# Adding the two directions' decay matrices on VectorE before the output matmuls of a state-space scan

## Chip, core and metric

One NeuronCore of one Trainium2 chip runs the whole kernel. The metric is the device time of one execution in microseconds (us); lower is better.

## What is computed

The kernel is one layer of a hybrid mixer on 1024 latent tokens with 256 context tokens as a prefix: one input projection, an HGRN2 branch (A), a Mamba-2 SSD branch (B), gates, an output projection and a layer norm. The change lies in branch B, where the sequence runs in both directions over chunks of 128 tokens. For each direction the reference computes, cut to what matters:

```python
cum = jnp.cumsum((dt * a_neg)...)
y_inter = jnp.einsum('bktgn,bktgr,bkgrnp->bktgrp', cc, jnp.exp(cum), s_prev)
cb = jnp.einsum('bktgn,bksgn->bktsg', cc, bc)
lmat = masked_exp(cum[:, :, :, None] - cum[:, :, None, :], causal)
y_intra = jnp.einsum('bktsg,bktsgr,bksgrp->bktgrp', cb, lmat, x_dt)
y = y_inter + y_intra          # per direction
...
y = y_f + y_b + d_skip * xh    # both directions
```

There are 16 heads of width 64 in 4 groups, and a state of 128. In `y_intra` both directions multiply the same tokens of x, each by its own matrix of 128 by 128.

## The kernel before

Projections are split-precision products: each weight tile of 128 columns is split into a high and a low part, and `mm3` (L178 to L180) issues three matmuls of 128x512 per 128 rows of contraction. These projections are also the fill work: `Fill.window` walks through the yields of a scan and after each one draws fill pieces until `due`, the yield's weight times the rate of the window, is used up. A piece counts its columns over 512, and one whole unit is 24 matmuls. The rates of the four group windows are `FILL_B`; the yield of a scan position counts `W_SCAN`, and that of a y step `W_Y`.

`b_scan` (from L793) handles one of the four groups. After the transposes and the masked product CB of B and C (L815), it makes nine positions of the state scan (xw L889 on GpSimd, bu L892 on TensorE, St L900 and L902 on VectorE), and then runs 16 y steps, two head pairs `j` times eight chunks `t`. A y step goes through four stages, at lags of 0, 2, 3 and 4 yields:

- `loads`: GpSimd issues a DMA (L837) that broadcasts the rows of cum of two heads and two directions into a tile L of 128x512.
- `exponents`: ScalarE makes e = exp(L) (L847); VectorE takes the minimum of L with CU (L848); ScalarE makes four exponentials of 128x128 in place (L851).
- `products`: GpSimd multiplies e by C (L856), VectorE multiplies L by CB (L857).
- `y_matmuls` (L859 to L875): eight matmuls into one PSUM tile yi, for k in 0..3 and the two heads h. k = 0, 1 multiply x by L of the two directions, k = 2, 3 multiply the states St by e. Heads h = 0 and 1 write different halves of 64 partitions. After four chunks VectorE adds d times x (L875).

L and e tiles share one pool of 12 buffers with other tiles, so a load waits until the matmuls of an earlier step have let a buffer go. The exact order on each engine is set by a list scheduler over this code, which takes program order, waits and priorities (`ahead`) into account. Beside the y steps the same engines serve the fill: ScalarE and VectorE split weights (L162, L163), run the convolution (L743, L746) and evacuate gates (L611, L925), and `b_out` and `b_scale` (L946 to L963) normalize the group before. ScalarE loads a function table (ACT_TABLE_LOAD) whenever the next function is not in the one it holds.

Of the kernel before, what the change touches and what calls it, by code (L numbers as in the profile page):

```python
# [14 lines left out]
NT = L // P  # L15
# [15 lines left out]
GRAIN = 512  # L31
FILL_T, FILL_A = 0.8, 0.8
GA = (2, 0, 0, 6)
FILL_B = (0.88, 0.97, 0.97, 1.05)
OUT1, OUT2 = 16, 3
GATES = (2, 1, 1, 4)
W_0, W_PRE, W_SCAN, W_Y = 1.0, 0.7, 0.35, 0.5
LAGS = (0, 2, 3, 4)
EARLY = (5, 7)
REP = 8  # L40
# [8 lines left out]
ALU = mybir.AluOpType  # L49
# [55 lines left out]
def hybrid(tc, x, c, ctx, c_ctx, w_mod, b_mod, w_in, lb_logits, a_norm_w, conv_w, conv_b, dt_bias,  # L105
# [4 lines left out]
    V, S, T, G = nc.vector, nc.scalar, nc.tensor, nc.gpsimd  # L110
# [8 lines left out]
    with root:  # L119
# [9 lines left out]
        def sc(name):  # L129
            return ps.tile([P, 512], F32, tag="sc", bufs=5, name=name)  # L130
# [602 lines left out]
        def bt_(tag, bufs, shape, name):  # L733
            return bp.tile([P] + list(shape), F32, tag=tag, bufs=bufs, name=name)
# [58 lines left out]
        def b_scan(g, u):  # L793
# [14 lines left out]
            for b in range(2):  # L808
                cb = sc(f"cb{g}_{b}")
                for i in range(4):  # L810
                    t = (b * 4 + i) * P
# [6 lines left out]
            xt = bt_("xt", 1, [NT, 2 * P], f"xt{g}")  # L818
# [34 lines left out]
            def products(j, t):  # L853
# [2 lines left out]
                G.tensor_tensor(C4, C4, Cc[:, ts].unsqueeze(1).broadcast_to([P, 4, P]), ALU.mult)  # L856
                V.tensor_tensor(Lm, Lm, CB[:, :, ts].unsqueeze(1).broadcast_to([P, 2, 2, P]), ALU.mult)  # L857

            def y_matmuls(j, t):  # L859
                Lm, Ce = Ls.pop((j, t)), Cs.pop((j, t))  # L860
                if t % 4 == 0:
                    yis[j] = sc(f"yi{g}_{j}_{t // 4}")
                yi = yis[j]
                o = slice((t % 4) * P, (t % 4 + 1) * P)
                for k in range(4):
                    for h in range(2):
                        hs = slice((2 * j + h) * 64, (2 * j + h + 1) * 64)
                        if k < 2:
                            a, r = xt[:, t, hs], Lm[:, h, k, :]
                        else:  # L870
                            a, r = St[:, t if k == 2 else NT - 1 - t, k - 2, hs], Ce[:, h, k - 2, :]
                        T.matmul(yi[h * 64:(h + 1) * 64, o], a, r, start=(k == 0), stop=(k == 3))  # L872
                if t % 4 == 3:
                    bs = slice((t - 3) * P, (t + 1) * P)
                    V.scalar_tensor_tensor(y[:, j, bs], xc[:, j, bs], bd_col(2 * g + j), yi, ALU.mult, ALU.add)  # L875


            St = bt_("St", 1, [NT, 2, 256], f"St{g}")
# [28 lines left out]
            for k in range(len(EARLY), len(steps) + LAGS[-1]):  # L907
                for lag, stage in zip(LAGS, (loads, exponents, products, y_matmuls)):
                    if 0 <= k - lag < len(steps):
                        stage(*steps[k - lag])  # L910
                yield W_Y
# [4 lines left out]
        def z_proj(g, u):  # L916
            for j in range(2):
                blk = 2 * g + j
                for t0, n, acc in (proj_k if blk == 2 * BG - 1 else proj)(O_Z + blk * P, parts_l, f"z{blk}"):
                    if acc is None:  # L920
                        yield n / GRAIN / 4
                        continue
                    with ahead():
                        zs = bt_("gb", 4, [512], f"z{blk}_{t0}")
                        S.activation(zs, acc, AF.Silu)  # L925
                    if g + 1 < BG:
                        z_mul(u, j, t0, zs)
                    else:
                        z_last.append((u, j, t0, zs))
                    yield n / GRAIN / 4  # L930
# [39 lines left out]
        def b_window(g):  # L970
            scan = b_scan(g, ub_[g])
            if g:
                yield from islice(scan, OUT1)
                yield from b_out(g - 1, ub_[g - 1])
                yield from islice(scan, OUT2)
                b_scale(g - 1, ub_[g - 1])
            yield from scan
# [11 lines left out]
        for g in range(BG):  # L989
# [9 lines left out]
            else:  # L999
                fill.add(z_proj(g, ub_[g]), f"z{g}")  # L1000
            fill.window(b_window(g), FILL_B[g])
            fill.until(f"b{g + 1}")
# [33 lines left out]
        with ExitStack() as st:  # L1036
# [40 lines left out]
            for nh in range(2):  # L1077
# [9 lines left out]
                for t in range(NT):  # L1087
# [8 lines left out]
                    r, bs = rr[t], st_[t]  # L1096
# [36 lines left out]
```

## Time and profile before

| what | us |
|---|---|
| median of the three runs | 1261.88 |
| the runs | 1260.83, 1261.88, 1946.27 |
| the profiled execution | 1258.42 |
| its span in the trace | 1256.6 |

The median is what a later time is compared with. The trace belongs to the profiled execution, which is 3.46 us under that median, and 1.8 us of it lie outside the span of the trace.

### The profile page before, as it was taken

The numbers are of one execution on the slowest core, as the hardware profiler recorded it, in microseconds if no ns is written. First come the engines' busy times: TensorE is split into PE (matmuls) and PEld (weight loads), VectorE is DVE, ScalarE is ACT, GpSimd is POOL, SyncE is SP. The second block draws the span as 40 slices with busy tenths as digits, with TensorE's granted clock in tenths as the row PEclk, the third lists the DMA queues.
The fourth block names the chain that finished last, engine by engine and source line by source line (L and its number), as shares of the span: only waits on it lengthen the run. The fifth ranks groups of instructions, "written<-read, shape, count | busy, mean of one in ns | idle before, by whom it ended". The sixth has DMA issues, their size and how long they took to land.

```text
span 1256.6 us, 18683 instructions
## 1 busy us (share of the span) xinstructions
PE 1225.9 (98%) x7624; PEld 994.4 (79%) x7624; DVE 775.4 (62%) x988; ACT 580.2 (46%) x926; POOL 197.1 (16%) x200
## 2 busy tenths in 40 slices
PE   5999999999999999999999999999999999999997
PEld 2778888788888888888788878877887778888885
DVE  2437744934644742569687677758765755575468
ACT  2436244434324323346954586467858862222010
POOL 1130000000000000005414261425053410000000
PEclk8999999999999999999999999999999999999999
DMA  9611212102112223113402241224233316654312
GB/s 317 201 42 49 53 35 94 44 18 69 35 34 70 60 68 111 51 34 93 135 26 59 68 151 33 69 71 140 82 104 110 126 51 234 241 211 141 119 42 101
DMA packets 115444, 119.14 MB, mean 95 GB/s; under 512 B 10320, under 2 KB 94992, under 8 KB 115360
## 3 DMA queue, kind: packets, MB, share of 16 engines
q1 hardware_dynamic: 105568, 101.04, 25.2%
q0 software_dynamic: 9440, 16.87, 4.7%
q8 instruction: 60, 0.98, 0.3%
q14 instruction: 24, 0.20, 0.1%
q10 hardware_dynamic: 352, 0.05, 0.0%
HBM read 98.77 MB, written 19.14 MB: 94 GB/s over the span
## 4 chain that ended last, share of the span: by engine, by line
PE 86%; ACT 5%; DVE 4%; issue 2%; DMA 1%; POOL 1%; SPq 0%; DVEq 0%; ACTq 0%; POOLq 0%
PE x L178 6%; PE x L179 5%; PE x L180 5%; PE yi L872 4%; PE f L180 3%; PE f L178 3%; PE f L179 3%; PE bu L892 2%; PE ga L178 2%; PE pl L520 2%; PE fo L180 2%; PE fo L179 2%; PE fo L178 2%; PE ga L180 2%; PE ga L179 2%; PE pb L179 2%
## 5 line engine op out<-in xcount | busy, mean ns | idle before, releaser
L856 POOL TENSOR_TENSOR e<-e,C 128x512 f32<-128x512 f32 x64 | 91.0, 1429 | 103.4 <-ACT e L847 103.0
L889 POOL TENSOR_TENSOR xw<-xtc,WU 128x512 f32<-128x512 f32 x8 | 8.7, 1112 | 584.3 <-ACT xtc L826 584.3
L851 ACT ACTIVATE L<-L,BIA 128x128 f32<-128x128 f32 x256 | 80.8, 390 | 36.8 <-DVE L L848 36.4
L848 DVE TENSOR_TENSOR L<-L,CU 128x512 f32<-128x512 f32 x64 | 77.3, 1231 | 9.6 <-ACT e L847 9.5
L857 DVE TENSOR_TENSOR L<-L,CB 128x512 f32<-128x512 f32 x64 | 55.5, 871 | 19.9 <-ACT L L851 19.6
L746 DVE SCALAR_TENSOR_TENSOR xc<-x,par,xc 128x496 f32<-128x496 f32 (+1 forms) x64 | 47.1, 735 | 21.4 <-ACT xc L743 20.3
L512 ACT COPY KX<-K 128x1024 f32<-128x1024 f32 x28 | 32.0, 1141 | 50.3 <-DVE K L531 45.2
L562 DVE SCALAR_TENSOR_TENSOR S<-S,T,ub 128x128 f32<-128x128 f32 x64 | 22.2, 347 | 51.4 <-ACT S L558 27.7
L178 PE MATMUL fo<-wo,mh 128*128 128x512 f32 x128 | 50.2, 392 | 0.0
L180 PE MATMUL fo<-wo,mh 128*128 128x512 f32 x128 | 49.8, 389 | 0.0
L179 PE MATMUL fo<-wo,ml 128*128 128x512 f32 x128 | 49.8, 389 | 0.0
L531 DVE TENSOR_TENSOR K<-K,T 128x1280 f32<-128x1280 f32 x28 | 46.4, 1658 | 3.4 <-ACT KX L512 1.6
L872 PEld LDWEIGHTS yi<-L,xt 128*64 128x64 f32 x512 | 26.7, 136 | 26.5 <-issue 18.9
L872 PE MATMUL yi<-L,xt 128*64 128x128 f32 x512 | 42.1, 285 | 3.5 <-issue 1.8
L837 POOL DMA_DIRECT2D L<-cum_d x64 | 39.7, 621 | 25.5 <-PE yi L872 10.8
L847 ACT ACTIVATE e<-L 128x512 f32<-128x512 f32 x64 | 37.4, 620 | 8.4 <-PE bu L892 3.9
L746 DVE SCALAR_TENSOR_TENSOR B<-x,par,B 128x496 f32<-128x496 f32 (+1 forms) x32 | 23.6, 736 | 28.5 <-ACT B L743 24.4
L533 DVE TENSOR_TENSOR Q<-Q,T 128x1024 f32<-128x1024 f32 x28 | 37.6, 1344 | 2.9 <-PE pl L520 2.9
L872 PE MATMUL yi<-e,St 128*64 128x128 f32 x512 | 38.9, 273 | 0.0
L520 PEld LDWEIGHTS pl<-Q,KX 128*64 128x64 f32 x896 | 30.1, 138 | 9.5 <-issue 8.7
L523 DVE COPY_PREDICATED PD<-mk,pl 128x512 f32<-128x512 uint8 x24 | 17.7, 739 | 27.9 <-PE pl L520 27.8
L520 PE MATMUL pl<-Q,KX 128*64 128x64 f32 x896 | 34.1, 230 | 0.7 <-DVE Q L533 0.7
(995 smaller groups left out, 3742.7 us busy)
## 6 DMA issues: line engine op xcount, KB each, us to landing
L<-cum_d POOLq DMA_DIRECT2D x64, 256.0 KB, 4.1
wm<-in_w_mod_dram SPq DMA_DIRECT2D x16, 512.0 KB, 8.2
xt<-in_x_dram SPq DMA_DIRECT2D x8, 512.0 KB, 8.2
ga_d<-ga SPq DMA_DIRECT2D x16, 256.0 KB, 2.0
gb_d<-gb SPq DMA_DIRECT2D x16, 256.0 KB, 3.9
m<-ga_d SPq DMA_DIRECT2D x8, 512.0 KB, 4.9
gbt<-gb_d SPq DMA_DIRECT2D x8, 512.0 KB, 6.7
wg<-in_w_mod_dram SPq DMA_DIRECT2D x8, 512.0 KB, 5.0
```

Source lines behind the costliest of these rows:

```text
L178: T.matmul(dst, ah, bh, start=(first and i == 0), stop=False)
L179: T.matmul(dst, al, bh, start=False, stop=False)
L180: T.matmul(dst, ah, bl, start=False, stop=(last and i == n - 1))
L520: T.matmul(pl[rows_, t * HP:(t + 1) * HP], KX[:, o:o + HP], qx, start=True, stop=True)
L531: V.tensor_tensor(kv, kv, sub(Ta, lv, [[w, NA // w], [NA - lv, 2], [0, lv]]), ALU.mult)
L746: V.scalar_tensor_tensor(d3[:, :, a:z], r3[:, :, a + o:z + o], cw_col(t, blk), d3[:, :, a:z], ALU.mult, ALU.add)
L837: G.dma_start(t_[:].rearrange("p a b c -> p (a b c)"), bass.AP(src.tensor, src.offset, [[NQT * BH * 2 * QT, REP], [0, P // REP], [1, 4 * Q ...
L848: V.tensor_tensor(Lm, Lm, sub(CU[:], t * BH + h0, [[1, 2], [NT * BH, 2], [0, P]]), ALU.min)
L851: S.activation(Lm[:, h, d, :], Lm[:, h, d, :], AF.Exp, bias=BIA[:, d, t, h0 + h:h0 + h + 1])
L856: G.tensor_tensor(C4, C4, Cc[:, ts].unsqueeze(1).broadcast_to([P, 4, P]), ALU.mult)
L857: V.tensor_tensor(Lm, Lm, CB[:, :, ts].unsqueeze(1).broadcast_to([P, 2, 2, P]), ALU.mult)
L872: T.matmul(yi[h * 64:(h + 1) * 64, o], a, r, start=(k == 0), stop=(k == 3))
```

## The change

The product L times CB is followed by one more VectorE instruction, which adds the two directions' halves of L (128x2x128 elements) in place. `y_matmuls` now runs k in 0..2: first the two products of St and e, then one product of x with the sum. Each y step thus has 6 matmuls where it had 8 (in the trace each of them stands as two instructions, so 12 for 16). The product of C with exp(cum) stays on GpSimd. The weight of a y step and the fill rates are changed as well.

```diff
-FILL_B = (0.88, 0.97, 0.97, 1.05)
+FILL_B = (0.85, 0.94, 0.94, 1.02)
-W_0, W_PRE, W_SCAN, W_Y = 1.0, 0.7, 0.35, 0.5
+W_0, W_PRE, W_SCAN, W_Y = 1.0, 0.7, 0.35, 0.54
...
                 V.tensor_tensor(Lm, Lm, CB[:, :, ts].unsqueeze(1).broadcast_to([P, 2, 2, P]), ALU.mult)
+                V.tensor_tensor(Lm[:, :, 0, :], Lm[:, :, 0, :], Lm[:, :, 1, :], ALU.add)
...
-                for k in range(4):
+                for k in range(3):
                     for h in range(2):
                         hs = slice((2 * j + h) * 64, (2 * j + h + 1) * 64)
                         if k < 2:
-                            a, r = xt[:, t, hs], Lm[:, h, k, :]
+                            a, r = St[:, NT - 1 - t if k else t, k, hs], Ce[:, h, k, :]
                         else:
-                            a, r = St[:, t if k == 2 else NT - 1 - t, k - 2, hs], Ce[:, h, k - 2, :]
-                        T.matmul(yi[h * 64:(h + 1) * 64, o], a, r, start=(k == 0), stop=(k == 3))
+                            a, r = xt[:, t, hs], Lm[:, h, 0, :]
+                        T.matmul(yi[h * 64:(h + 1) * 64, o], a, r, start=(k == 0), stop=(k == 2))
```

In the changed file the lines after the added one stand two lower (L872 is L874, L953 is L955), and the added instruction is L859.

TensorE, group 1, the step of j = 0 and t = 5. L and e are the step's tiles, xt the tokens of x, St the states, and gb and x are fill. Before:

```order
L180 MATMUL gb_512_5917<-hl_95,gb2h 128x512
L872 MATMUL yi_0_1_5941<-L_0_5_5764,xt_5432 64x128 x4
L872 MATMUL yi_0_1_5941<-e_0_5_5899,St_5494 64x128 x4
L178 MATMUL x_0_5996<-hh_80,x4h 128x512
L179 MATMUL x_0_5996<-hh_80,x4l 128x512
```

Now:

```order
L180 MATMUL x_0_5951<-hl_89,x4h 128x512
L874 MATMUL yi_0_1_5929<-e_0_5_5888,St_5478 64x128 x4
L874 MATMUL yi_0_1_5929<-L_0_5_5742,xt_5416 64x128 x2
L178 MATMUL x_0_5951<-hh_82,x4h 128x512
L179 MATMUL x_0_5951<-hh_82,x4l 128x512
```

The L matmuls moved behind the four of e, and two of them are gone. Over the whole program TensorE has 6093 matmuls where it had 6221; the 64 steps stood in 64 unbroken runs and stand in 72, since fill now comes between the e and the L matmuls of some steps.

VectorE, the same place. Before:

```order
L857 TENSOR_TENSOR L_0_4_5725<-L_0_4_5725,CB_5398 128x512
L848 TENSOR_TENSOR L_0_5_5764<-L_0_5_5764,CU 128x512
L848 TENSOR_TENSOR L_0_6_5863<-L_0_6_5863,CU 128x512
L875 SCALAR_TENSOR_TENSOR xc_5042<-xc_5042,par,yi_0_0_5736 128x512
L963 SCALAR_TENSOR_TENSOR xc_4242<-xc_4242,par,sq_1_1_5855 128x512
L857 TENSOR_TENSOR L_0_5_5764<-L_0_5_5764,CB_5398 128x512
L857 TENSOR_TENSOR L_0_6_5863<-L_0_6_5863,CB_5398 128x512
```

Now:

```order
L857 TENSOR_TENSOR L_0_4_5701<-L_0_4_5701,CB_5382 128x512
L965 SCALAR_TENSOR_TENSOR xc_4242<-xc_4242,par,sq_1_1_5838 128x512
L848 TENSOR_TENSOR L_0_5_5742<-L_0_5_5742,CU 128x512
L859 TENSOR_TENSOR L_0_4_5701<-L_0_4_5701 128x2x128
L848 TENSOR_TENSOR L_0_6_5852<-L_0_6_5852,CU 128x512
L965 SCALAR_TENSOR_TENSOR xc_4242<-xc_4242,par,sq_1_1_5838 128x512
L877 SCALAR_TENSOR_TENSOR xc_5035<-xc_5035,par,yi_0_0_5713 128x512
L857 TENSOR_TENSOR L_0_5_5742<-L_0_5_5742,CB_5382 128x512
L859 TENSOR_TENSOR L_0_5_5742<-L_0_5_5742 128x2x128
L857 TENSOR_TENSOR L_0_6_5852<-L_0_6_5852,CB_5382 128x512
```

The add L859 follows its product L857 directly, or with one instruction between.

ScalarE, group 1, where `b_out` of group 0 (sq and bss) meets the step of t = 4. Before:

```order
L847 ACTIVATE e_0_4_5865<-L_0_4_5725 128x512
L953 ACT_TABLE_LOAD
L953 ACTIVATE sq_0_1_5840<-bss_0_5850,epsr 128x512
L953 ACTIVATE sq_1_1_5855<-bss_1_5859,epsr 128x512
L954 ACT_TABLE_LOAD
L954 ACTIVATE sq_0_1_5840<-sq_0_1_5840 128x512
L954 ACTIVATE sq_1_1_5855<-sq_1_1_5855 128x512
L851 ACTIVATE L_0_4_5725<-L_0_4_5725,BIA 128x128 x4
L847 ACTIVATE e_0_5_5899<-L_0_5_5764 128x512
```

Now:

```order
L847 ACTIVATE e_0_4_5854<-L_0_4_5701 128x512
L955 ACT_TABLE_LOAD
L955 ACTIVATE sq_0_1_5823<-bss_0_5833,epsr 128x512
L956 ACT_TABLE_LOAD
L956 ACTIVATE sq_0_1_5823<-sq_0_1_5823 128x512
L851 ACTIVATE L_0_4_5701<-L_0_4_5701,BIA 128x128 x3
L955 ACT_TABLE_LOAD
L955 ACTIVATE sq_1_1_5838<-bss_1_5848,epsr 128x512
L851 ACT_TABLE_LOAD
L851 ACTIVATE L_0_4_5701<-L_0_4_5701,BIA 128x128
L956 ACTIVATE sq_1_1_5838<-sq_1_1_5838 128x512
L847 ACTIVATE e_0_5_5888<-L_0_5_5742 128x512
```

The two halves' logarithm and exponential no longer go together, which makes four table loads of two; group 2 shows the same. Over the whole program ScalarE has 109 table loads where it had 97, the added ones 4, 4, 2 and 2 in the windows of groups 0 to 3.

## Rows read from the trace of the kernel before

**Rows 1.** Page, span, and busy time, share and instructions of each engine

```profile
span 1256.6 us, 18683 instructions
PE 1225.9 (98%) x7624; PEld 994.4 (79%) x7624; DVE 775.4 (62%) x988; ACT 580.2 (46%) x926; POOL 197.1 (16%) x200
```

**Rows 2.** Busy time by stretch, the y steps of the four groups

```profile
core 0: us, PE busy (x) PEld busy (x) DVE busy (x) ACT busy (x) POOL busy (x), PEclk, DMA share, GB/s
597.00:655.00 58.00, 58.00 (x437) 44.62 (x436) 42.82 (x48) 42.29 (x85) 20.30 (x20) 1.00 0.29 87
724.00:778.00 54.00, 52.81 (x393) 40.92 (x394) 43.15 (x53) 44.25 (x85) 22.89 (x22) 1.00 0.34 103
846.00:901.00 55.00, 52.47 (x394) 40.68 (x393) 44.22 (x53) 44.47 (x85) 22.07 (x21) 1.00 0.36 110
965.00:1020.00 55.00, 54.76 (x384) 41.36 (x384) 40.65 (x38) 47.59 (x87) 20.10 (x19) 1.00 0.40 125
sum 222.00, PE 218.04 PEld 167.58 DVE 170.85 ACT 178.60 POOL 85.36; mean PE 54.51 PEld 41.89 DVE 42.71 ACT 44.65 POOL 21.34
```

**Rows 3.** Waits for line L872: TensorE idle until VectorE's product, us and times

```profile
  DVE L L857: 5.5, 8
```

**Rows 4.** Timeline of TensorE, one y step of group 0: start, us, what, count

```profile
621.98 0.39 PE L180 MATMUL x<-hl,x2h 128*128 128x512 f32 x1
622.30 0.66 PE L872 MATMUL yi<-L,xt 128*64 128x128 f32 x8
622.79 0.61 PE L872 MATMUL yi<-e,St 128*64 128x128 f32 x8
623.33 0.50 PE L178 MATMUL x<-hh,x2h 128*128 128x512 f32 x1
623.66 0.40 PE L179 MATMUL x<-hh,x2l 128*128 128x512 f32 x1
```

**Rows 5.** Chain that ended last, in time: a fill matmul, then 20 transposes

```profile
562.20 0.23 PE x L180
562.43 2.18 PE bx L825 x20
```

**Rows 6.** Page, groups of the y step's instructions: busy, mean ns, idle before

```profile
L856 POOL TENSOR_TENSOR e<-e,C 128x512 f32<-128x512 f32 x64 | 91.0, 1429 | 103.4 <-ACT e L847 103.0
L848 DVE TENSOR_TENSOR L<-L,CU 128x512 f32<-128x512 f32 x64 | 77.3, 1231 | 9.6 <-ACT e L847 9.5
L857 DVE TENSOR_TENSOR L<-L,CB 128x512 f32<-128x512 f32 x64 | 55.5, 871 | 19.9 <-ACT L L851 19.6
```

**Rows 7.** Line L848: ns min, median and max of its 64 instructions

```profile
L848 DVE TENSOR_TENSOR L<-L,CU x64: 673/692/3994, 576.9 to 1007.2; 128x512 f32<-128x512 f32 x64
```

**Rows 8.** Groups by shape on VectorE: the same operation at 512 and 1024 elements

```profile
L338 DVE TENSOR_TENSOR hl<-hm,hh 128x512 fp32r<-128x512 f32 x8 | 5.5, 690 | 0.2
L163 DVE TENSOR_TENSOR ml<-m,mh 128x1024 fp32r<-128x1024 f32 x8 | 9.8, 1226 | 0.3 <-ACT mh L162 0.3
```

**Rows 9.** Groups in 560:1060: one of ScalarE's groups of table loads

```profile
L851 ACT ACT_TABLE_LOAD x21 | 26.9, 1283 | 0.3
```

**Rows 10.** Timeline of ScalarE in group 1, from the logarithm of group 0

```profile
723.92 0.63 ACT L847 ACTIVATE e<-L 128x512 f32<-128x512 f32 x1
724.57 1.28 ACT L953 ACT_TABLE_LOAD   x1
725.87 1.26 ACT L953 ACTIVATE sq<-bss,epsr 128x512 f32<-128x512 f32 x2
...
739.38 0.63 ACT L847 ACTIVATE e<-L 128x512 f32<-128x512 f32 x1 [0.86 <-POOL e L856]
...
750.95 1.28 ACT L851 ACTIVATE L<-L,BIA 128x128 f32<-128x128 f32 x4 [0.92 <-DVE L L848]
...
755.94 1.28 ACT L851 ACTIVATE L<-L,BIA 128x128 f32<-128x128 f32 x4 [3.19 <-DVE L L848]
```

**Rows 11.** Timeline of VectorE in group 1: the product of t = 5

```profile
736.34 0.69 DVE L857 TENSOR_TENSOR L<-L,CB 128x512 f32<-128x512 f32 x1 [1.66 <-ACT L L851]
```

**Rows 12.** Timeline of TensorE in group 1: the matmuls of t = 5

```profile
737.47 0.66 PE L872 MATMUL yi<-L,xt 128*64 128x128 f32 x8
```

## Prediction

> **What bounds the kernel now.** I began with the page's busy shares. TensorE is busy 1225.9 of 1256.6 us, VectorE 62% and ScalarE 46% [rows 1]. The end of the program is therefore set by TensorE's stream, and an instruction taken from it is worth its own slot as long as nothing makes TensorE wait. The second view, busy time by stretch, tells whether that holds where the change lies. In the four stretches of y steps, 222.0 us together, TensorE is busy 218.04 us at the full granted clock (1.00, the 2.4 GHz level), but the helpers are far busier than over the whole program: ScalarE 178.6 us (80%), VectorE 170.85 us (77%) [rows 2]. The third view, the waits of the y matmuls, shows the coupling: TensorE sits idle until VectorE's product L857 only 8 times in 64 steps, 5.5 us in all [rows 3]. So TensorE bounds, and VectorE and ScalarE stand close behind it in these stretches.
>
> **TensorE: what is removed.** The trace shows each y matmul as two instructions. A step starts its L part at 622.30, its e part at 622.79 and the next fill matmul at 623.33 [rows 4]: eight L instructions take 0.49 us, 61 ns each. Half of them go, 4 x 61 = 0.245 us a step, and 64 steps give 15.7 us. A slot, not the duration of 0.66 us that the row prints, is the price, since the instructions overlap. It cannot be read from matmuls that use all output columns: the 20 transposes of 128 columns take 2.18 us, 109 ns each [rows 5]. The y matmuls of the two heads write different halves and run nearly side by side; since a whole pair is removed and pairs remain, 61 ns is the price of one. What bounds it from both sides are these two rows: 61 ns (15.7 us) and 109 ns (27.9 us). I take the first, which is the row of the very instructions.
>
> **TensorE: what is added.** The program's order has 72 runs of y matmuls where it had 64. Entering a run costs 622.30 - 621.98 = 0.32 us where a fill matmul follows its neighbour by 0.23 [rows 4, 5], and leaving it 623.66 - 623.33 = 0.33, again 0.10 more. A further run thus costs 0.19 us, and 8 of them 1.6 us. TensorE's stream becomes 15.7 - 1.6 = 14.1 us shorter.
>
> **The fill rates** add or remove no work, they move it. A unit of fill is 24 matmuls of 0.23 us, 5.5 us. Per y step the due work goes from 0.88 x 0.5 = 0.44 units to 0.85 x 0.54 = 0.459 in group 0, from 0.485 to 0.508 in groups 1 and 2, from 0.525 to 0.551 in group 3: 0.10, 0.12, 0.12 and 0.14 us a step. Over 16 steps in each group 8.0 us of fill go from the scan positions to the y steps. The y stretches become 222.0 - 15.7 + 1.6 + 8.0 = 215.9 us long. Should the fill run out before the last step, steps would stand back to back. In group 3 the window's yields weigh 15.67 (5.55 up to the scan's end, 18 y yields of 0.54, 0.4 of `b_out`), times 1.02 is 15.98 units of 16 at hand, where it was 15.70; it just suffices, so I cost it at nothing.
>
> **VectorE: the add.** No row shows a TENSOR_TENSOR of 256 elements. 512 elements take 690 ns and 1024 take 1226 [rows 8], 1.05 ns an element, so 256 take about 0.42 us when nothing disturbs. Disturbed it is longer: L848 has a median of 692 ns and a mean of 1231, with one of 3994, and its neighbour L857, of the same shape, a mean of 871 [rows 6, 7]. So a y step's VectorE instruction loses 0.18 us (L857) to 0.54 us (L848) on average; the add costs 0.42 at least, 0.60 like its neighbour, 0.96 like L848. A bound below nothing is excluded, since it replaces no other VectorE instruction. I take 0.60, since L859 stands directly behind L857 in the order. 64 adds are then 38.4 us (27 to 61). VectorE's load in the y stretches becomes 170.85 + 38.4 = 209.3 of 215.9 us: it fits, with hardly anything to spare. In the order the added instruction delays what is queued behind it, the next L848 and L857, and by them ScalarE's L851.
>
> The cover of the add is the new order of the matmuls. L is now needed after the e part, 0.49 us later than before. Where TensorE waited for the product already, 8 steps, an add of 0.60 shows by 0.60 - 0.49 = 0.11 us, 0.9 us in all. The step at 737.47 has 0.44 us to spare after its product, which ends at 736.34 + 0.69 [rows 11, 12], and becomes one of that kind; GpSimd's e products, which now come first, I cost at nothing: GpSimd is busy 85 of the 222 us [rows 2], and no wait for it is among those of the y matmuls.
>
> What disturbs L848 is told by the trace only as durations. The Trainium skill, SBUF — State Buffer, section "Who interferes with whom", states that a VectorE instruction with two SBUF inputs contends with a GpSimd one that reads SBUF, and that the loser waits for the whole instruction. The long L848 agree. By that rule the add, with both inputs in SBUF, can wait for a whole L856; the rule speaks against the change, and the last rival below is its result.
>
> **ScalarE: the table loads.** The order holds 12 further table loads, at 1.283 us each [rows 9]. A load at 724.57 follows the instruction that started at 723.92 and lasted 0.63, and the next starts at 725.87 [rows 10]: a switch costs 1.30 us and nothing more. Whether it shows depends on ScalarE's gaps. From 723.92 to 750.0 in group 1 it has one gap of 0.86 us, then 0.92 and 3.19 [rows 10]; the two loads added there, between logarithm and exponential, are 2.6 us ahead of the step at 737.47 with its 0.44 us. I let them show in full, and likewise in group 2, where the order is the same: 2 x 2.6 = 5.1 us. The other eight lie in group 0, where no TensorE time is lost now [rows 2], or at the windows' ends, and I cost them at nothing; uncovered they are 10.3 us.
>
> The Trainium skill, ScalarE: Activation LUTs, section "What ACT_TABLE_LOAD costs", gives 2.66 us for a switch, with a drain behind the load. The trace does not agree here: 1.30 us from load to next start. By the page these four loads would be 10.6 us in place of 5.1, and I go by the row.
>
> **The sum.** -15.7 + 1.6 + 5.1 + 0.9 = -8.1 us. The profiled execution took 1258.42 us, so 1250.3; its median of runs lies 3.46 higher, and so do I: 1253.8 us.
>
> **Rivals.**
> *All covered.* Of the 222 us, 51 us of VectorE's and 43 us of ScalarE's time are idle [rows 2]. If neither term shows, the gain is TensorE's 14.1 us: 1247.8 us. Against it stand ScalarE's unbroken stretch and the small slack in rows 11 and 12.
> *ScalarE paces the steps.* All 12 loads show, 15.4 us against 14.1: 1263.2 us, no change. For it speaks ScalarE's 80%; against it that groups 0 and 3 lose 0.24 us of TensorE time together now [rows 2].
> *VectorE becomes the bound.* If each add costs what L848 loses, 0.96 us, VectorE needs 170.85 + 61.4 = 232.3 us in stretches that could be 215.9, and TensorE waits for the 16.4 us: 1261.88 - 14.1 + 16.4 = 1264.2 us, slower than before. It decides from (215.9 + 14.1 - 170.85) / 64 = 0.92 us an add. For it: L848's mean. Against it: L857, two places nearer, loses a third of that, and waiting for GpSimd can't grow beyond GpSimd's own 85 us.
> *The removed matmuls are worth a full slot.* At 109 ns the gain is 27.9 - 1.6 = 26.3 us, 1235.6 us. Rows 4 speak against it. That the change does not do what it says is excluded by the order: 128 matmuls fewer.
>
> **How the numbers follow.** Forecast 0.48; all covered 0.25; ScalarE 0.13; VectorE 0.12; full slot 0.02. The predicted time is the forecast's, 1253.8 us. The range runs from 1245 (all covered, with the adds' and loads' bounds at nothing and 3 us of TensorE's present waits gone) to 1266 (past both slower cases), and leaves out the full slot and a pileup of both slower cases. About 2% is what a measurement of this kernel can tell from no change, 25 us: faster by that is only the full slot, 0.02; slower would need VectorE's case at twice its price, 0.03; within it 0.95.
>
> **What would show it.** In the changed profile L874 should have 512 e and 256 L instructions with slots of 61 ns; L859 a mean of 0.4 to 1.0 us; TensorE's idle time in the y stretches 4 us before and about 10 after, most of it in groups 1 and 2 and released by L859. TensorE's busy time should fall by 14 us. If TensorE's idle time stays at 4 us, the ScalarE and VectorE terms were wrong; if it grows by 14 or more, their cover was. A VectorE above 97% busy in these stretches would mean the third rival.

## The result and the profile after

The changed kernel takes 1277.21 us (median of 4 runs, 1273.85 to 1278.55), the kernel before beside it 1260.83: a ratio of 1.0129, interval 1.0116 to 1.0142. One slow run of the kernel before, 1946.27 us, is left out of these figures. The change makes the kernel slower by 16.4 us, where 1253.8 was forecast and 1266 was the upper end. The profiled execution of after took 1273.85 us.

First the page, span and busy time, against [rows 1].

```profile
span 1272.1 us, 18243 instructions
PE 1224.2 (96%) x7368; PEld 986.9 (78%) x7368; DVE 798.6 (63%) x1052; ACT 598.8 (47%) x938; POOL 195.1 (15%) x200
```

The span grew by 15.5 us. TensorE's busy time fell by only 1.7 us although 256 of its matmul instructions (128 matmuls) are gone, and its idle time (span less busy) rose from 30.7 to 47.9, by 17.2. Those two make the 15.5. Where the idle time lies is told by the same four stretches as in [rows 2] (busy time by stretch).

```profile
597.00:655.00 58.00, 51.84 (x320) 38.67 (x319) 44.08 (x55) 44.02 (x86) 20.09 (x20) 0.94 0.28 87
724.00:778.00 54.00, 49.42 (x296) 36.68 (x294) 43.93 (x55) 45.09 (x80) 23.81 (x24) 0.97 0.35 108
846.00:901.00 55.00, 50.42 (x302) 37.83 (x301) 43.43 (x53) 45.62 (x82) 24.75 (x24) 0.97 0.38 118
965.00:1020.00 55.00, 47.58 (x261) 33.74 (x261) 34.07 (x35) 41.57 (x69) 21.32 (x21) 0.94 0.40 123
sum 222.00, PE 199.27 PEld 146.91 DVE 165.51 ACT 176.30 POOL 89.96; mean PE 49.82 PEld 36.73 DVE 41.38 ACT 44.08 POOL 22.49
```

TensorE idles 22.7 us of the 222 where it idled 4.0: 18.8 us more, so all of the added idle time is here. VectorE is busy 165.5 us, 75%, no more than before (170.85): it is not full. The granted clock, 1.00 in all four rows before, is 0.94 to 0.97. If the loss is taken as one minus this clock times the stretch, it is 3.48 + 1.62 + 1.65 + 3.30, an estimate of some 10 us of TensorE's time. That is why the busy time hardly fell: the y matmuls take 11.9 us less (worked out below, in the part on why the prediction was wrong), the clock gives 10 us back.

Next come the waits of the y matmuls, first in the kernel before, then in the changed one (behind the add the lines stand two higher, L872 is L874). [rows 3] is another view: its 5.5 us in 8 add up three waits of matmuls (1.7 us) and five of weight loads (3.8 us), and leave out the wait put down to "issue". TensorE's matmuls waited 3.5 us in four before, and 22.7 us in ten now, and the waits hardly name an engine. The groups of VectorE and GpSimd answer to [rows 6], with the added instruction L859, and the source view gives the least, median and greatest duration of L859.

```profile
PE yi L872 <- issue: 1.8, 1, 1.8
PE yi L872 <- DVE L L857: 1.7, 3, 0.8
```

```profile
PE yi L874 <- issue: 19.7, 9, 3.4
PE yi L874 <- ACT z6h L162: 3.0, 1, 3.0
```

```profile
L856 POOL TENSOR_TENSOR e<-e,C 128x512 f32<-128x512 f32 x64 | 88.6, 1389 | 135.5 <-ACT e L847 134.9
L848 DVE TENSOR_TENSOR L<-L,CU 128x512 f32<-128x512 f32 x64 | 66.6, 1044 | 9.4 <-ACT e L847 9.2
L857 DVE TENSOR_TENSOR L<-L,CB 128x512 f32<-128x512 f32 x64 | 51.4, 803 | 23.2 <-ACT L L851 23.1
L859 DVE TENSOR_TENSOR L<-L 128x256 f32<-128x256 f32 x64 | 48.9, 764 | 0.8
```

```profile
L859 DVE TENSOR_TENSOR L<-L x64: 410/425/3568, 588.8 to 1035.5; 128x256 f32<-128x256 f32 x64
```

The one wait put down to ScalarE ends at 991.80, and the add before it ran from 988.14 to 991.70: it is L859's as well. The add's mean is 764 ns, but few adds are like that mean: 48 of the 64 take less than 0.5 us, and the longest take up to 3.57 us. One of these is in group 0; here are VectorE, GpSimd and TensorE around it in the timeline (start, us, engine, line; an idle time stands in brackets).

```profile
615.87 3.57 DVE L859 TENSOR_TENSOR L<-L 128x256 f32<-128x256 f32 x1
615.99 1.30 POOL L856 TENSOR_TENSOR e<-e,C 128x512 f32<-128x512 f32 x1
617.22 0.63 POOL L837 DMA_DIRECT2D L<-cum_d  x1
617.87 1.27 POOL L856 TENSOR_TENSOR e<-e,C 128x512 f32<-128x512 f32 x1
619.53 0.44 PE L874 MATMUL yi<-L,xt 128*64 128x128 f32 x4 [2.62 <-issue]
```

The add lies over two whole GpSimd products and the DMA issue between them, and ends 0.30 us after the second. TensorE, which asked for the sum at 616.91, starts 0.09 us after the add's end. An undisturbed add (425 ns) would have been ready at 616.30, in time. So the wait that the view puts down to "issue" is a wait for L859. The second example, in group 1, is the stretch for which the prediction charged the table loads.

```profile
735.25 1.28 ACT L955 ACT_TABLE_LOAD   x1
736.54 0.69 ACT L955 ACTIVATE sq<-bss,epsr 128x512 f32<-128x512 f32 x1
737.25 1.28 ACT L851 ACT_TABLE_LOAD   x1
738.54 0.41 ACT L851 ACTIVATE L<-L,BIA 128x128 f32<-128x128 f32 x1
738.98 0.69 DVE L857 TENSOR_TENSOR L<-L,CB 128x512 f32<-128x512 f32 x1 [3.19 <-ACT L L851]
739.59 0.75 DVE L965 SCALAR_TENSOR_TENSOR xc<-xc,par,sq 128x512 f32<-128x512 f32 x1
740.15 1.31 POOL L856 TENSOR_TENSOR e<-e,C 128x512 f32<-128x512 f32 x1 [6.46 <-ACT e L847]
740.25 1.75 DVE L848 TENSOR_TENSOR L<-L,CU 128x512 f32<-128x512 f32 x1
741.92 1.69 DVE L859 TENSOR_TENSOR L<-L 128x256 f32<-128x256 f32 x1
742.05 1.28 POOL L856 TENSOR_TENSOR e<-e,C 128x512 f32<-128x512 f32 x1
743.72 0.44 PE L874 MATMUL yi<-L,xt 128*64 128x128 f32 x4 [3.45 <-issue]
```

ScalarE's exponential comes late behind the loads, so L857 waits 3.19 us. Then L965 and L848 are queued on VectorE between the product and the add; L848 and the add, 1.75 and 1.69 us, are each held over a GpSimd product. TensorE idles 3.45 us.

All ten waits end when L859 is done, but the add itself is held in only some of them. Three waits (619.53, 991.80 and 1008.26; 8.3 us) follow adds of 3.55 to 3.57 us. Two (743.72 and 867.23; 6.9 us) follow adds of 1.69 us that came late as well. One (636.91; 3.3 us) follows an add of 0.83 us behind an L857 that was held for 3.80 us. Four (4.2 us) follow undisturbed adds of 0.41 us that came late; at 773.13 and 896.63 four other VectorE instructions stood between the product and the add.

What TensorE does after the 3.45 us is the third part of the loss.

```profile
744.93 0.63 PE L178 MATMUL gb<-hh,gb2h 128*128 128x512 f32 x1
745.36 0.63 PE L179 MATMUL gb<-hh,gb2l 128*128 128x512 f32 x1
...
748.63 0.66 PE L874 MATMUL yi<-e,St 128*64 128x128 f32 x8
749.12 0.39 PE L874 MATMUL yi<-L,xt 128*64 128x128 f32 x4
749.43 0.50 PE L178 MATMUL x<-hh,x4h 128*128 128x512 f32 x1
```

```profile
745.00:748.50 3.50, 3.50 (x10) 0.54 0.74 266
```

From 744.93 fill matmuls follow one another by 0.43 us in place of 0.23, and TensorE's own row of 745 to 748.5 shows a granted clock of 0.54, the 1.2 GHz level for nearly all of it. TensorE had idled until 743.72. At 748.63 it is back, and an unhindered step reads 0.49 us for the e part and 0.31 for the L part: 0.80 from 748.63 to 749.43, against 1.03 before [rows 4].

### The profile page after: what moved, and what is told of

It is laid out like the page before. It is cut to its first block, busy times and chain, and to the rows that moved or that the text cites. A ratio compares the mean times of both kernels' runs of the same rounds, so it can differ in the third digit from the quotient of the medians.

```text
span 1272.1 us, 18243 instructions
## 1 busy us (share of the span) xinstructions
PE 1224.2 (96%) x7368; PEld 986.9 (78%) x7368; DVE 798.6 (63%) x1052; ACT 598.8 (47%) x938; POOL 195.1 (15%) x200
## 4 chain that ended last, share of the span: by engine, by line
PE 87%; DVE 5%; ACT 5%; issue 2%; DMA 1%; POOL 0%; SPq 0%; DVEq 0%; ACTq 0%
PE x L178 6%; PE x L179 6%; PE x L180 5%; PE yi L874 4%; PE f L180 3%; PE f L178 3%; PE z L178 3%; PE f L179 2%; PE ga L178 2%; PE z L180 2%; PE pl L520 2%; PE z L179 2%; PE pb L180 2%; PE pb L179 2%; PE fo L178 2%; PE pb L178 2%
## 5 line engine op out<-in xcount | busy, mean ns | idle before, releaser
L848 DVE TENSOR_TENSOR L<-L,CU 128x512 f32<-128x512 f32 x64 | 66.6, 1044 | 9.4 <-ACT e L847 9.2
L857 DVE TENSOR_TENSOR L<-L,CB 128x512 f32<-128x512 f32 x64 | 51.4, 803 | 23.2 <-ACT L L851 23.1
L562 DVE SCALAR_TENSOR_TENSOR S<-S,T,ub 128x128 f32<-128x128 f32 x64 | 22.3, 348 | 51.4 <-ACT S L558 27.7
L859 DVE TENSOR_TENSOR L<-L 128x256 f32<-128x256 f32 x64 | 48.9, 764 | 0.8
L874 PE MATMUL yi<-L,xt 128*64 128x128 f32 x256 | 27.0, 288 | 23.0 <-issue 19.7
L874 PEld LDWEIGHTS yi<-e,St 128*64 128x64 f32 x512 | 28.4, 140 | 19.7 <-issue 16.1
L874 PE MATMUL yi<-e,St 128*64 128x128 f32 x512 | 42.9, 289 | 0.0
L874 PEld LDWEIGHTS yi<-L,xt 128*64 128x64 f32 x256 | 15.7, 139 | 30.1 <-issue 25.1
```

The lines of the kernel that those rows point to most:

```text
L848: V.tensor_tensor(Lm, Lm, sub(CU[:], t * BH + h0, [[1, 2], [NT * BH, 2], [0, P]]), ALU.min)
L859: V.tensor_tensor(Lm[:, :, 0, :], Lm[:, :, 0, :], Lm[:, :, 1, :], ALU.add)
```

## Experiments

Three theories were set against each other. P: VectorE's instruction with two inputs is held while a GpSimd product runs, so single sums are late at the moment when TensorE wants them. C: the add is simply more work than VectorE has time for in the y stretches. L: ScalarE's added table loads, which come with the new fill rates, make everything late. Ratios are to the kernel before on the same chip. The rounds ran on different chips, where the kernel before took 1259.7 to 1260.8 us, so a difference of times from two rounds is uncertain by about 1 us.

**The fill rates alone and undone.** In the change (old_rates) and in the kernel before (rates_only):

```diff
old_rates, from the change:
-FILL_B = (0.85, 0.94, 0.94, 1.02)
+FILL_B = (0.88, 0.97, 0.97, 1.05)
-W_0, W_PRE, W_SCAN, W_Y = 1.0, 0.7, 0.35, 0.54
+W_0, W_PRE, W_SCAN, W_Y = 1.0, 0.7, 0.35, 0.5
rates_only, from the kernel before: the reverse
```

> The changed kernel with the fill rates and the y step's weight of before. Theories: (P, port) the add L859, with two inputs in SBUF, waits for GpSimd's products L856, and stands where TensorE waits for it; (L, loads) the new rates made an order with 12 more table loads on ScalarE, and these pace the steps; (C, capacity) VectorE simply has too much work in the y stretches. The order has 99 table loads here (97 before, 109 in the changed kernel). P: waits of 2 to 4 us for L859 stay, TensorE idle in the y stretches over 10 us, 1266 to 1280 us. L: the loss goes, 1248 to 1256 us. C: as P, 1270 us or more.

> The kernel before with only the fill rates and the y step's weight of the changed kernel; 105 table loads in the order. P: there is no add, so 1256 to 1265 us. L: 8 more loads without TensorE's saving, 1266 to 1274 us. C: as P.

Measured: old_rates 1267.75 us, 1.0062 (1.0047 to 1.0077); rates_only 1261.15 us, 1.0011 (1.0002 to 1.0020). Both lie in P's ranges and outside L's; old_rates is also under C's 1270. L859 still has a mean of 758 ns in old_rates, and TensorE's y matmuls still wait 16.7 us in seven waits of up to 4.0 us, three of them put down to "issue" (groups and waits in 560 to 1060):

```profile
L859 DVE TENSOR_TENSOR L<-L 128x256 f32<-128x256 f32 x64 | 48.5, 758 | 0.9
```

```profile
PE yi L874 <- issue: 7.9, 3, 4.0
```

So the add with its matmul order loses even at the old rates, which L can't explain; but the new rates cost 9.5 us on top of it (8.4 by the ratios), and only 1.0 us in the kernel before. The two make each other dearer.

**The add left out.** The kernel no_add, and no_add_old with the old rates, leave out the backward direction's part within a chunk (its decay matrix is computed and never used); the 256 matmul instructions stay out as in the change.

```diff
-                V.tensor_tensor(Lm[:, :, 0, :], Lm[:, :, 0, :], Lm[:, :, 1, :], ALU.add)
no_add_old besides: FILL_B and W_Y of before, as in old_rates
```

> The changed kernel without the add; y takes only the forward direction's half of L, so the backward direction's part within a chunk is left out. 107 table loads in the order. P: TensorE's saving of 14 us shows, 1243 to 1250 us, and TensorE never waits over 1.5 us in the y stretches. C: the same. L: the loads stay, 1262 us or more.

> The changed kernel without the add (the backward direction's part within a chunk left out), with the fill rates of before and GpSimd's product; 97 table loads as in the kernel before. If the waits of 1260.7 us without the add came from GpSimd's products alone (P): 1255 to 1262 us, TensorE still waits 6 us or more for the product L857. If the new rates and their 10 loads made them (L): TensorE's saving of 11 us shows, 1247 to 1252 us.

Measured: no_add 1260.73 us, 1.0002 (0.9993 to 1.0012); no_add_old 1254.79 us, 0.9961 (0.9946 to 0.9976). The add costs 16.5 us at the new rates and 13.0 at the old. But without it the full gain does not appear either: no_add misses P's 1243 to 1250 by 11 us and lies 1.3 us under L's 1262 or more. no_add_old lies between the two again, 0.2 us under P's range and 2.8 us above L's, and TensorE waits there 3.7 us for L857 where P wanted 6 or more. The waits and L848's group of no_add say why:

```profile
PE yi L873 <- DVE L L857: 14.0, 10, 2.4
```

```profile
L848 DVE TENSOR_TENSOR L<-L,CU 128x512 f32<-128x512 f32 x64 | 86.8, 1373 | 9.8 <-ACT e L847 9.7
```

The hold is back on L848 (mean 1373 ns) and reaches TensorE through L857, 14.0 us where the y matmuls waited 3.5 in all in the kernel before. A reading that fits is that the faster steps ask sooner for a product that comes no sooner; no run shows it by itself.

**GpSimd's product moved to VectorE.** This takes away what holds VectorE and gives VectorE 64 further instructions. In the change (eprod_v), in the kernel before (eprod_v_before), in the change with the add left out as above (eprod_v_noadd), and in the change with the old rates (eprod_v_old):

```diff
-                G.tensor_tensor(C4, C4, Cc[:, ts].unsqueeze(1).broadcast_to([P, 4, P]), ALU.mult)
+                V.tensor_tensor(C4, C4, Cc[:, ts].unsqueeze(1).broadcast_to([P, 4, P]), ALU.mult)
eprod_v_noadd besides:
-                V.tensor_tensor(Lm[:, :, 0, :], Lm[:, :, 0, :], Lm[:, :, 1, :], ALU.add)
eprod_v_old besides: FILL_B and W_Y of before, as in old_rates
```

> The changed kernel with the product of C and exp(cum) on VectorE in place of GpSimd: 64 instructions of 128x512 more for VectorE (about 0.69 us each undisturbed, 44 us), and nothing on GpSimd that reads SBUF in the y steps. P: L848, L857 and L859 all come down to their undisturbed 0.69, 0.69 and 0.42 us, TensorE's waits go, 1244 to 1254 us. C: VectorE has still more work, 1285 us or more. L: no change against the changed kernel, 1270 to 1280 us.

> The kernel before with the product of C and exp(cum) on VectorE; 97 table loads, 8 matmuls in a step, no add. Port (P): VectorE no longer waits for GpSimd, L848 and L857 fall to 0.69 us, and TensorE's 3.5 us of waits go, but its matmuls stay: 1256 to 1261 us. So the 9 us of the changed kernel with this edit come from the matmuls and need the edit only to show. If instead the edit itself were worth the 9 us, whatever the matmuls: 1249 to 1253 us. Capacity (C): 44 us more VectorE work, 1262 us or more.

> The changed kernel with the product of C and exp(cum) on VectorE and without the add (the backward direction's part within a chunk is left out). It has no GpSimd product and no add: TensorE's saving alone. P: the add undisturbed is covered, so within 2 us of the 1251.2 us with the add. C: VectorE has 27 us less work than with the add, 1245 us or less.

> The changed kernel with the product of C on VectorE and the fill rates of before; 102 table loads against 107. On GpSimd the old rates were worth 9.5 us (1267.75 against 1277.21). If the rates count only by where GpSimd's products fall and what they hold up (P), they count for little here: within 3 us of 1251.2. If they count by the table loads (L): 5 us or more below it, 1246 us or less.

Measured: eprod_v 1251.19 us, 0.9930 (0.9914 to 0.9947); eprod_v_before 1254.98, 0.9961 (0.9947 to 0.9975); eprod_v_noadd 1245.94, 0.9890 (0.9875 to 0.9904); eprod_v_old 1248.00, 0.9904 (0.9887 to 0.9920). The groups of eprod_v:

```profile
L856 DVE TENSOR_TENSOR e<-e,C 128x512 f32<-128x512 f32 x64 | 44.5, 704 | 0.0
L857 DVE TENSOR_TENSOR L<-L,CB 128x512 f32<-128x512 f32 x64 | 44.1, 689 | 19.5 <-ACT L L851 19.0
L848 DVE TENSOR_TENSOR L<-L,CU 128x512 f32<-128x512 f32 x64 | 43.9, 687 | 10.8 <-ACT e L847 10.8
L859 DVE TENSOR_TENSOR L<-L 128x256 f32<-128x256 f32 x64 | 27.0, 421 | 0.7
```

Each of the four instructions runs at its undisturbed time. Their sum is 159.5 us for 256 instructions, where the 192 of the change took 66.6 + 51.4 + 48.9 = 166.9: one instruction more a step, and VectorE is less busy. That refutes C. The 107 table loads that this run keeps, of the change's 109, refute L as the main cause. Four waits of the y matmuls are left, 4.1 us in all.

The other three runs missed what P expected, though none by much. The add still costs 5.3 us (1251.2 against 1245.9 without it), where P had allowed 2 and C 6 or more: even undisturbed it is not wholly covered. eprod_v_before lies 1.0 us under P's range, so the edit by itself gives 4.7 us in the kernel before, about half of the 9.0 us by which eprod_v beats that kernel. eprod_v_old lies 0.2 us outside P's 3 us and short of L's 1246 or less. It is faster than both kernels of the case: 12.0 us under the one before.

**Half of it.** GpSimd makes the product in even chunks only (eprod_alt):

```diff
-                G.tensor_tensor(C4, C4, Cc[:, ts].unsqueeze(1).broadcast_to([P, 4, P]), ALU.mult)
+                (V if t % 2 else G).tensor_tensor(C4, C4, Cc[:, ts].unsqueeze(1).broadcast_to([P, 4, P]), ALU.mult)
```

> The changed kernel with the product of C on VectorE in the odd chunks and on GpSimd in the even ones; 109 table loads as in the changed kernel. P: half of GpSimd's products hold VectorE half as much: L848, L857 and L859 lose less than half of their 51 us, and the time lies between 1251.2 and 1277.2, at 1258 to 1268 us. L: 1270 us or more, as the loads are those of the changed kernel.

Measured: 1256.49 us, 0.9974 (0.9965 to 0.9984), better than P's range. The mean of L859 is 600 ns and that of L848 889, so a hold remains, but the longest L859 is 2.30 us where it was 3.57 (the longest L848 is 2.24 in both). All 109 table loads of the change are there, which speaks against L once more. Four fifths of eprod_v's gain on the change come with half the move: 20.7 of 26.0 us.

**The add in other forms.** With a tile of its own for the sum, so that it waits for nothing but its inputs (add_sep); the same as a reduction, which has one input (reduce_sep; it sums both directions of the same product); and on GpSimd (add_g):

```diff
add_sep and reduce_sep (W has 11 buffers where it had 12, y_matmuls read Ss):
-                V.tensor_tensor(Lm[:, :, 0, :], Lm[:, :, 0, :], Lm[:, :, 1, :], ALU.add)
+                Ss[j, t] = bt_("ls", 2, [2, P], f"ls{g}_{j}_{t}")
+                V.tensor_tensor(Ss[j, t], Lm[:, :, 0, :], Lm[:, :, 1, :], ALU.add)
reduce_sep, in place of the last line:
+                V.tensor_reduce(Ss[j, t], Lm[:].rearrange("p h d t -> p h t d"), mybir.AxisListType.X, ALU.add)
add_g:
+                G.tensor_tensor(Lm[:, :, 0, :], Lm[:, :, 0, :], Lm[:, :, 1, :], ALU.add)
```

> The changed kernel with the sum written to a tile of its own (the shared pool has 11 buffers in place of 12, two tiles are added for the sums). Control for the next: the add still has two inputs in SBUF. P: single adds of 2 to 4 us, mean 0.65 us or more, 1268 to 1280 us. C: the same.

> As the control, but the sum is a TENSOR_REDUCE over the two directions: one input of 512 elements in place of two of 256, undisturbed about 0.69 us against 0.42, 17 us more of VectorE time over 64 steps. P: no instance above 1 us, since one input does not need what GpSimd holds; the waits go over to L848, as without the add, so 1258 to 1266 us, at least 4 us under the control. C: more VectorE work, 3 us or more above the control.

> The changed kernel with the add on GpSimd, behind its products; 107 table loads. VectorE loses 49 us of work in the y steps. P: GpSimd has 64 more instructions that read SBUF, so L848 and L857 lose as much as in the changed kernel or more, and the sums wait in GpSimd's queue: 1262 to 1285 us. C: VectorE has room, 1258 us or less.

Measured: add_sep 1268.24 us, 1.0067 (1.0052 to 1.0082); reduce_sep 1269.71, 1.0074 (1.0054 to 1.0095); add_g 1268.28, 1.0063 (1.0047 to 1.0079). The source views of add_sep and of reduce_sep, least, median and greatest:

```profile
L860 DVE TENSOR_TENSOR ls<-L x64: 403/424/3597, 589.5 to 1027.5; 128x256 f32<-128x256 f32 x64
```

```profile
L860 DVE TENSOR_REDUCE ls<-L x64: 679/696/714, 590.1 to 1031.5; 128x256 f32<-128x512 f32 x64
```

Same place, same queue, same GpSimd beside it: the instruction with two inputs is held up to 3.6 us, that with one input never takes more than 18 ns over its median, though 15 of the 64 overlap a GpSimd product. The Trainium skill, SBUF — State Buffer, section "Who interferes with whom", states this: with two SBUF inputs a VectorE instruction contends with a GpSimd one that reads SBUF, and a reduction does not. These runs agree. Yet the kernel is no faster with the reduction. The means suggest why: the holds stay on L848 (mean 1223 ns, 1150 in add_sep), and the work itself grows by 64 x 0.27 = 17 us. P had said 4 us under add_sep and C 3 us or more above it; both were wrong. With the add on GpSimd VectorE does exactly the work of before, and TensorE waits nearly as long as in the change, now for GpSimd:

```profile
PE yi L874 <- POOL L L859: 19.4, 15, 3.7
```

It counts against C again: VectorE has nothing more to do than before, and the kernel takes 1268 us where C said 1258 or less.

**The y matmuls one step later.** Whether the loss is lateness or a want of throughput was still open, as the holds had moved to L848 in two runs and TensorE waited all the same. With the same instructions, the y matmuls of a chunk are issued one step later behind its products: in the change (lag5), in the kernel before (lag5_before), in eprod_v_old (lag5_ev_old).

```diff
-LAGS = (0, 2, 3, 4)
+LAGS = (0, 2, 3, 5)
```

> The change with the y matmuls one step later behind their products (LAGS 0, 2, 3, 5 in place of 0, 2, 3, 4). Nothing is computed less or more; 105 table loads in place of 109. Theory P (lateness: the sum comes 1 to 3.5 us after TensorE asks for it, behind two or three GpSimd products, and a step lasts about 3.4 us): TensorE's waits for L859 fall from 21 us to under 5, the stretches at the half clock between 597 and 1020 go, L848, L857 and L859 keep their means (1044, 803, 764 ns within a tenth), and the time is 1246 to 1256. Theory C (VectorE or ScalarE has too much to do in these stretches for the rate of the steps, so a wait moves but does not go): TensorE still idles 15 us or more, and the time is 1268 to 1282.

> The kernel before with the y matmuls one step later (LAGS 0, 2, 3, 5); the control of the run above. Theory P: only the 5.5 us of waits for L857 can go, 1254 to 1262. Theory C: no difference, 1258 to 1264.

> The change with the C product on VectorE, the fill rates of before, and the y matmuls one step later (100 table loads): whether the two remedies add. Theory P: with the product on VectorE the sum no longer waits, TensorE idles under 1 us there, so a later step gives nothing: 1245 to 1250. Theory C: a lower rate of demand on VectorE at the y steps helps further, under 1244.

Measured: lag5 1261.27 us, 1.0007 (0.9995 to 1.0019); lag5_before 1254.89, 0.9961 (0.9948 to 0.9974); lag5_ev_old 1248.51, 0.9907 (0.9891 to 0.9924). One more step of slack gives the change 16.0 us back, while L848 is held longer than in the change and L857 and L859 somewhat less (means 1122, 735, 638 ns against 1044, 803, 764): it was lateness in the main, and C's 1268 or more is out. P's range is missed too, by 5 us: eight waits of 1.3 to 2.9 us, 14.3 us in all, remain in the y stretches, where P had said under 5. The granted clock of the four stretches is 0.97, 1.00, 1.00 and 1.00, by the reckoning above 1.7 us lost where the change lost 10; so about half of what lag5 gains is waits, and half is clock. One of the waits in lag5's timeline:

```profile
631.54 1.29 POOL L856 TENSOR_TENSOR e<-e,C 128x512 f32<-128x512 f32 x1
...
633.41 2.52 POOL L856 TENSOR_TENSOR e<-e,C 128x512 f32<-128x512 f32 x2
```

```profile
631.80 4.70 DVE L848 TENSOR_TENSOR L<-L,CU 128x512 f32<-128x512 f32 x1
...
637.62 0.41 DVE L859 TENSOR_TENSOR L<-L 128x256 f32<-128x256 f32 x1
```

```profile
638.14 0.59 PE L874 MATMUL yi<-L,xt 128*64 128x128 f32 x4 [2.94 <-ACT L L851]
```

L848 is held for 4.70 us by three products in a row. L859 at 637.62, though itself undisturbed, comes behind it on VectorE, and TensorE waits 2.94 us. A hold of three products is longer than the step that was given (about 3.4 us). In lag5_before no wait of a y matmul is left and TensorE is busy 222.00 of the 222 us; there 5.3 us are gained (3.3 to 6.6 by the interval), and TensorE's idle time in these stretches was 4.0. In lag5_ev_old the later step adds nothing to 1248.0: in eprod_v_old TensorE was busy 221.87 of the 222 us already, so both remedies act on the same microseconds.

## Why the prediction was wrong

**VectorE, the add: the step that failed.** Its price was put at 0.60 us with ends at 0.42 and 0.96; 0.764 was measured, inside. What failed is the cover, that TensorE's 0.49 us stand against 0.60 and 0.11 us show, 0.9 us in all. Instead TensorE waited 22.7 us for L859 in ten waits, where the y matmuls had waited 3.5. A mean was set against a slack, though the rows of that step already showed a median of 692 ns, a mean of 1231 and a longest of 3994 [rows 6, 7]. The holds come in lumps of one to three GpSimd products, and a cover of half a microsecond hides none of them. TensorE's idle time in the y stretches grew by 18.8 us where 0.9 + 5.1 were allowed. The prediction's own test (growth of 14 or more: the cover was wrong) points to this step.

Two readings led there. The 8 steps and 5.5 us of [rows 3] count weight loads with the matmuls; and the longest wait of a y matmul before, the 1.8 us put down to "issue", is not among them. It ends at 877.19, just after an L857 that was held over three products:

```profile
872.13 2.54 POOL L856 TENSOR_TENSOR e<-e,C 128x512 f32<-128x512 f32 x2
872.66 4.43 DVE L857 TENSOR_TENSOR L<-L,CB 128x512 f32<-128x512 f32 x1
875.25 1.27 POOL L856 TENSOR_TENSOR e<-e,C 128x512 f32<-128x512 f32 x1
```

So the trace of before already showed a lump that reached TensorE. And L859 does not always stand directly behind L857, or with one instruction between: the listing under "The change" has L965 and L848 between the two of t = 4, and in the trace 24 adds follow their product directly, 30 with one instruction between, and 10 with two to four. (By the prediction's own figures the step at 737.47 had 0.44 + 0.49 us for an add of 0.60 and would not have become one that waits.)

**What holds VectorE.** "Waiting for GpSimd can't grow" was nearly right and did not help. Taken as busy time over 64 medians, L848 and L857 (by the 690 ns of the same shape) lost (77.3 - 44.3) + (55.5 - 44.2) = 44.3 us before; L848, L857 and L859 lose 22.8 + 7.4 + 21.7 = 51.9 after. Not the sum changed so much as its place: 21.7 us of it now lie on the last instruction before TensorE.

**The rival "VectorE becomes the bound"** told the right sign by a wrong mechanism: VectorE was to be over 97% busy and is 75%, and the add is under the 0.92 us from which this rival was to decide. eprod_v and add_g refute it. The rule of the port was cited as speaking against the change, with this rival as its result (the prediction calls it the last, but it is the third). Contention with GpSimd's product was the cause; the error was to let it act through VectorE's load alone.

**TensorE, -14.1 us.** Right in kind, too large by 2 us or more. A step's matmuls take 0.80 us against 1.03: 64 x 0.23 = 14.7 for the forecast 15.7. A step split by fill takes 0.37 for the L part (743.72 to 744.09 in the timeline) and 0.59 for the e part (613.73 to 614.32) in place of 0.80, 0.16 more. The 0.19 for entering and leaving a run, all that was taken, comes on top: 0.35 a split, 2.8 us for eight in place of 1.6 (8 x 0.19 is 1.5). That leaves 11.9. In no_add_old, with the old rates, as many matmuls as the change and a granted clock of 1.00 in all four stretches, TensorE's busy time is 1215.5 us, 10.4 under the kernel before. In the change this is given back in idle time and clock. With GpSimd's product off, eprod_v_noadd stands 9.0 us under eprod_v_before; the two differ in their fill rates as well.

**The clock** had no term. Its 10 us come out of four stretches, each at or right after one of the six waits of 2.6 us or more, so a long wait can cost more than its length. This share is read from the windows, in lag5 too; no run held the clock apart.

**The fill rates and table loads, +5.1 us.** Too small here, and not a constant. The steps that were charged are those of the waits at 743.72 and 867.23, 6.9 us together, which late exponentials and held VectorE instructions share. The medians side by side:

| | rates of before | new rates |
|---|---|---|
| kernel before | 1260.2 | 1261.2 |
| without the add, product on GpSimd | 1254.8 | 1260.7 |
| the change | 1267.8 | 1277.2 |
| the change, product on VectorE | 1248.0 | 1251.2 |

The rates cost 9.5 us in the change, 5.9 without the add, 3.2 with the product on VectorE, 1.0 in the kernel before. What they cost depends on the slack that the rest leaves. How much of it is loads, and how much another placing of GpSimd's products beside VectorE's instructions, stays open: no run changed the loads at a fixed order. Nor did a run have the new order of the y matmuls without the removed ones; in the change no y matmul waited for GpSimd's e product, as the prediction had it.

## What to carry to other kernels

Set a cover against the longest duration that a row shows, or against its lumps, not against the mean: a median of 692 ns beside a mean of 1231 says that the cost comes as some holds of microseconds. Before an instruction with two inputs is added between a GpSimd product and TensorE, try the kernel with that product moved to VectorE; here 64 more VectorE instructions made VectorE less busy and the kernel 26 us faster. Where a wait remains, one step more between producer and consumer keeps a buffer longer and gave 5 us in the kernel before and 16 in the changed one.

## What the runs showed of the hardware

Two GpSimd products in a row had a DMA issue of 0.63 us between them, and a held VectorE instruction was let in there at times and at times not. L848 at 740.25 ended at 742.00, between the products of 740.15 and 742.05. The add at 615.87 lasted 3.57 us over two products, and L848 in lag5 4.70 us over three. The three longest adds of the change, 3.55 to 3.57 us, had each started 0.12 or 0.13 us before a product and lasted over that one and the next. TensorE's clock went to the 1.2 GHz level after some idle times of about 3 us in the midst of dense work (0.54 in 745 to 748.5, after 3.45 us of idle), where the kernel before shows 1.00 in all four stretches. After other waits of that length it did not fall: the waits of 2.62 us before 619.53 and of 3.01 us before 991.80 left it at 1.00, as fill matmuls 0.23 us apart show there.
